# A hybrid decoder layer on one core: the order of TensorE's products turned, in the middle of each up-projection chunk and in the mixer

## The chip, the core and the metric

One core of one Trainium2 chip. The metric is device time in microseconds (us) of one execution; lower is better. The profile is taken from one execution of its own, and its span runs from the first to the last instruction.

## What is computed

One decoder layer on a sequence of 256 tokens of width 2048, in float32:

```python
h = rms_norm(x, mix_norm_g)
q, kv, gate_logits, conv_in = split(h @ w_in)
attn = nsa_attention(q, kv, sigmoid(gate_logits), ...)   # three gated branches, 16 heads of 64
conv = conformer_conv(conv_in, ...)                      # GLU, causal depthwise conv of 31 taps, LayerNorm, swish
x = x + concatenate([attn, conv]) @ w_out
h = rms_norm(x, ffn_norm_g)
u = causal_depthwise_conv(h @ w_up, ffn_conv_w, ffn_conv_b)   # 3 taps, 2 x 5632 channels
a, gate = split(u)
x = x + (silu(gate) * a) @ w_down
return rms_norm(x, final_norm_g)
```

## The kernel before

**Products in two halves.** Every operand of a large product is split into a high part, rounded to the matmul's reduced float32 form (`wh` for a weight, `xt_h` for an activation), and the rest (`wl`, `xt_l`). A product is then the sum of three: high x high, high weight x low activation, low weight x high activation. The three are accumulated in a PSUM bank, so their order is free as long as the first one starts the sum and the last one stops it. A product of TensorE has an operand that is kept (it is loaded ahead as weights, a record of its own on the row PEld) and one that streams; the width in the profile's forms (128x256, 128x512) is that of the streaming one.

**Weight chunks.** All weights stream through SBUF in chunks of 128 x 2048. The list `chunks` counts them: 0 to 2 are the head (loaded in pieces), 3 to 23 the convolution's and the keys' columns of `w_in`, 24 to 29 the values' and gates', 30 to 37 the queries', then the output projection, then 88 chunks of `w_up` and 44 of `w_down`. For each chunk the sync queue starts the load into `wraw` (3 buffers), ScalarE makes `wh` (L207), and VectorE or, for chunks 5 to 31, GpSimd makes `wl` as `wraw - wh` (L212), each in two halves in the mixer. `w_next` hands a chunk to TensorE, adds one to `st["use"]`, and writes the splitting of the chunk two ahead; the pieces are put into ScalarE's and the subtracting engine's queues in the middle of TensorE's work. There are 3 buffers of `wh` and `wl`. The order of instructions on each engine is that in which the program writes them.

**The mixer.** `tile_chunk` (L492) takes a chunk of 128 output columns and calls `mm3` (L244) for each of the 16 rows of tiles; each call issues three products of width 256 with the weight kept: `wh` x `xt_h` (L245), `wh` x `xt_l` (L246), `wl` x `xt_h` (L247). `hook` in between puts in other engines' work and ticks of the attention. At the very start the head's three chunks arrive in ten cuts (`CUTS`, `THIRD`); its products are written at L567 for the first cuts and by `mm3` for the rest, 38 calls; chunks 3 to 23 and 30 to 37 make 29 x 16 more calls. The values' products (L827 to L829) and the output projection's (L262 to L264) keep the activation and stream the weight.

**The up-projection.** For each of 22 groups m, two parts (a and gate) and two halves kh of the sum, one chunk holds 8 rows of tiles k for 2 output tiles i. Each pair (k, i) issues a product of width 512 (L1360: `wh` kept, the high and the low activation streaming side by side into the two halves of bank `bk[i]`) and one of width 256 (L1362: `wl` kept, the high activation into the first half). So the two widths take turns, and the banks change after each pair. `up_out` adds the halves of the bank afterwards, applies the three taps and the gate, and the down-projection (L254 to L257) follows.

Of the kernel before, what the change touches and what calls it, by code (L numbers as in the profile page):

```python
# [17 lines left out]
P = 128  # L18
T = 256
D = 2048  # L20
KD = D // P
# [22 lines left out]
CUTS = ((0, 1), (1, 2), (2, 4), (4, 5), (5, 6), (6, 8), (8, 10), (10, 12), (12, 14), (14, 16))  # L44
THIRD = {1: (0, 2), 2: (2, 4), 4: (4, 6), 5: (6, 8), 9: (8, 16)}
EARLY = 4


def head_of_slot(s):
# [5 lines left out]
def hybrid_trunk(ctx: ExitStack, tc: tile.TileContext, a: dict, out: bass.AP):  # L55
    nc = tc.nc
# [39 lines left out]
        presums.extend(lambda i=i: nc.gpsimd.dma_start(far, src[:, i * 512:(i + 1) * 512],  # L96
                                                       **({"accum_op": OP.add} if i else {})) for i in (0, 1, 3))

    st = {"dma": 3, "split": 3, "use": 0}
    raws, parts, pieces, halves = {}, {}, [], []  # L100
    late, lows, late_pool, far_sums, out_sums = [], [], [], {}, []
    clock = {"pe": 0.0, "dve": 0.0}
# [120 lines left out]
    def w_next(cuts=1, ahead=LA):  # L223
        c = st["use"]
        st["use"] += 1
        w_pump()
        if st["split"] >= len(chunks):
            for f in lows:
                f()
            lows.clear()  # L230
        while st["split"] <= min(c + ahead, len(chunks) - 1):
            w_pump()
            w_split(cuts)
        if cuts == 1 or POOLED[0] <= st["split"] - 1 < POOLED[1]:
            w_pump()
        now = late[:]
        late.clear()
        if now:
            clock["dve"] = max(clock["dve"], clock["pe"])
        for f in now:  # L240
            f()
        return parts.pop(c)

    def mm3(ps, wh, wl, xh, xl, first, last):  # L244
        nc.tensor.matmul(ps, wh, xh, start=first, stop=False)  # L245
        nc.tensor.matmul(ps, wh, xl, start=False, stop=False)  # L246
        nc.tensor.matmul(ps, wl, xh, start=False, stop=last)  # L247
        clock["pe"] += 0.36

    def mm_down(ps, xh, xl, wh, wl, first, last):  # L250
# [48 lines left out]
    xt = [mixp.tile([P, 4, 2, T], F32R, name="xt", bufs=4) for _ in range(4)]  # L299
    xt_h, xt_l = [[xt[k // 4][:, k % 4, i] for k in range(KD)] for i in range(2)]  # L300


    with ExitStack() as mx:
# [24 lines left out]
        for n, (lo, hi) in enumerate(CUTS):  # L328
            w = 512 * (hi - lo)
# [5 lines left out]
            if n in THIRD:  # L335
                sl = slice(*[k * P for k in THIRD[n]])
# [30 lines left out]
        for n, ((lo, hi), (xc, *wc)) in enumerate(zip(CUTS, heads)):  # L367
            xs = [(xc[:, (k - lo) * T:(k - lo + 1) * T], k) for k in range(lo, hi)]
            sl = slice(lo * P, hi * P)
            if n < EARLY:  # L370
                h, l = parts[0]
# [13 lines left out]
            if n in THIRD:  # L385
                sl = slice(*[k * P for k in THIRD[n]])
# [105 lines left out]
        def tile_chunk(ps, ticks={}, half=None):  # L492

            wh, wl = w_next(2)
            held = pieces[:] if half else []
            del pieces[:len(held)]
            for kt in range(KD):
                if kt == KD // 2 and half:
                    half()
                    pieces.extend(held)  # L500
                if kt % 4 == 2:
                    hook(kt // 4, ticks)
                sl = slice(kt * P, (kt + 1) * P)
                mm3(ps, wh[:, sl], wl[:, sl], xt_h[kt], xt_l[kt], kt == 0, kt == KD - 1)
# [53 lines left out]
        for j in range(8):  # L558
            gb, ab = [b[:, :T] for b in bank[2 * (j if j < 3 else (j + 1) % 2):][:2]]
            if j == 0:  # L560
                st["use"] = 3
                ps3 = gb, ab, bank[2][:, :T]
                for n, cut in enumerate(CUTS):
                    if n < EARLY:
                        for c, i, j in ((0, 0, 0), (0, 1, 0), (1, 0, 0), (0, 0, 1), (1, 0, 1), (1, 1, 0)):
                            for k in range(*cut):
                                nc.tensor.matmul(ps3[c], parts[c][i][:, k * P:(k + 1) * P], (xt_h, xt_l)[j][k],  # L567
                                                 start=k + i + j == 0, stop=False)
                                clock["pe"] += 0.12
                    for c, (lo, hi) in ((0, cut), (1, cut), (2, THIRD.get(n, (0, 0)))):  # L570
                        wh, wl = parts[c]
                        for k in range(lo, hi) if c == 2 or n >= EARLY else ():
                            sl = slice(k * P, (k + 1) * P)
                            mm3(ps3[c], wh[:, sl], wl[:, sl], xt_h[k], xt_l[k], k == 0, k == KD - 1)
                for c in range(3):
                    parts.pop(c)
                w_split(2)
                w_pump()
                x_squares(0, 0)
                x_squares(0, 1)  # L580
                w_split(2)
                pieces[1:3] = pieces[2:0:-1]
                w_pump(2)
                x_squares(1, 0)
                x_rstd()
                w_pump()
                first = gb, ab
                continue
# [115 lines left out]
        for n in range(4):  # L704
            kv, i = divmod(n, 2)
# [111 lines left out]
        for kh in range(2):  # L817
            wh, wl = [w.rearrange("p (k c) -> p k c", c=256) for w in w_next(2)]
            presum_step()
            for k in range(8):  # L820
                kt = kh * 8 + k
                if k % 2 == 1:
                    hook(k // 2)
                for t in range(2):
                    sl = slice(t * P, (t + 1) * P)
# [7 lines left out]
        for kq in range(4):  # L833
            wh, wl = [w[:, :4 * 304].rearrange("p (k c) -> p k c", c=304) for w in w_next(2)]
            for k in range(4):
                kt = kq * 4 + k
                hook(k)
                for t in range(2):
                    sl = slice(t * P, (t + 1) * P)
# [285 lines left out]
        def x2_tr(qr, t):  # L1125
            for k in range(4 * qr, 4 * qr + 4):
                nc.tensor.matmul(x2_at(k)[:, t * P:(t + 1) * P], x2[:, t, k * P:(k + 1) * P], ident,
                                 is_transpose=True, start=True, stop=True)

        def x2_evac(k):  # L1130
            norm_evac(x2_at(k), k, ffn_g)
# [80 lines left out]
    with ExitStack() as fx:  # L1212
# [19 lines left out]
        def g_load():  # L1232

            n = gn["n"]
            gn["n"] += 1
            if n >= NFT // 2:
                return
            q = n % (NFT // 4)
            gl = fw.tile([P, 8, P], F32R, name="gl", bufs=2)
            nc.gpsimd.dma_start(gl.bitcast(F32), gl_far[q])  # L1240
            gq.append((gh_all[:, 4 * q:4 * q + 4].rearrange("p k a t -> p (k a) t"), gl))
# [26 lines left out]
        def sum_steps():  # L1268

            for q in sums_todo[2::-1]:  # L1270
                if len(q) == 3 and any(len(r) == 3 for r in sums_todo[:sums_todo.index(q)]):
                    continue
                q.pop(0)()
            while sums_todo and not sums_todo[0]:
                sums_todo.pop(0)
# [58 lines left out]
        def up_stages():  # L1334
            for q in list(stages):
                q.pop(0)()
                if not q:
                    stages.remove(q)


        for t in range(2):
            x2_rstd(t)
        between = {(0, 1): lambda: x2_tr(3, 0), (0, 8): w_pump, (0, 9): lambda: x2_tr(3, 1),
                   (0, 10): lambda: (x2_evac(12), x2_evac(13)),
                   (0, 12): lambda: (x2_evac(14), x2_evac(15)), (1, 8): x2_spread}

        for m in range(NFT // 2):
            ya = {}
            if m == NFT // 2 - 1:
                for _ in range(2):  # L1350
                    g_load()
            for part in range(2):
                bk = UP_BANKS[2 * ((2 * m + part) % 4):][:2]
                for kh in range(2):
                    wh, wl = [w.rearrange("p (k c) -> p k c", c=256) for w in w_next(1 if m + part + kh else 2)]
                    up_stages()
                    for n, (k, i) in enumerate((k, i) for k in range(8) for i in range(2)):
                        kt = kh * 8 + k
                        sl = slice(i * P, (i + 1) * P)
                        nc.tensor.matmul(bk[i], wh[:, k, sl], xt[kt // 4][:, kt % 4].rearrange("p a t -> p (a t)"),  # L1360
                                         start=kt == 0, stop=False)
                        nc.tensor.matmul(bk[i][:, :T], wl[:, k, sl], xt_h[kt], start=False, stop=kt == KD - 1)  # L1362
                        if m + part == 0 and (kh, n) in between:
                            between.pop((kh, n))()
                up_out(m, part, bk, ya)
                sum_steps()

# [148 lines left out]
        for h in range(2):  # L1516
            nb = dict(zip((2, 3, 4, 8, 1, 5, 6, 7), ring[4 * h:] + ring[:4 * h]))
            for q in range(NQ):
# [11 lines left out]
                for j in range(2):  # L1530
                    p = 2 * q + j
# [102 lines left out]
```

## Time and profile before

| | |
|---|---|
| three runs, median (lowest to highest) | 1083.47 us (1083.26 to 1083.47) |
| the profiled execution's own time | 1083.45 us |
| its span | 1081.7 us |
| granted TensorE clock, mean | 0.999 |
| up-projection, first to last product (L1360, L1362) | 353.4 to 847.2 us |
| mixer's `mm3` products (L245, L246, L247) | 502 of each |

In the profile PE is TensorE's matmuls and PEld its weight loads, DVE VectorE, ACT ScalarE, POOL GpSimd and SP the sync engine. A row of the timeline has the start, the length, the engine, the line, the operation, and the tiles as out<-in. A matmul's length holds its way through the array and overlaps the next one's; what a product costs is the distance from its start to the next start.

### The profile page before, as it was taken

To read this page: it belongs to the slowest core of one execution; us is meant where nothing else is said; L and a number is where in the kernel's file an instruction comes from. 1 tells how busy PE (TensorE), PEld (TensorE's weight loads), DVE (VectorE), ACT (ScalarE), POOL (GpSimd) and SP (SyncE) were. 2 spreads that over 40 slices of the span, in tenths; PEclk is the share of its full clock that TensorE was granted. 3 is DMA by queue.
4 is the path that set the end of the run, shared out by engine and by line. 5 is a ranking of instruction groups with operands and counts; after the bars stand their busy time and mean duration, and the time that the engine had idled before them with its cause. 6 is when DMAs were issued, how large, how long until landed. Compare 5 with 4: busy or idle time off the path is not lost.

```text
span 1081.7 us, 17521 instructions
## 1 busy us (share of the span) xinstructions
PE 1071.9 (99%) x6721; PEld 956.4 (88%) x6721; DVE 897.7 (83%) x1429; ACT 620.2 (57%) x895; POOL 368.0 (34%) x420
## 2 busy tenths in 40 slices
PE   9999999999999999999999999999999999999997
PEld 9999999998888888888888888888888888888886
DVE  6799986787895677777787878888787899999997
ACT  7534456778664545555455655555555555555563
POOL 0888975758000202333323433211121222211220
PEclk9999999999999999999999999999999999999999
DMA  9776756322565969999999999866668699979882
GB/s 354 243 262 253 222 145 237 115 90 107 198 219 206 279 213 277 272 290 262 307 278 292 287 289 301 272 217 219 224 224 270 210 394 343 345 287 351 324 314 99
DMA packets 62016, 272.82 MB, mean 252 GB/s; under 512 B 8187, under 2 KB 11531, under 8 KB 42348
## 3 DMA queue, kind: packets, MB, share of 16 engines
q1 hardware_dynamic: 34748, 199.33, 51.3%
q0 software_dynamic: 23536, 65.29, 22.6%
q10 hardware_dynamic: 3648, 7.08, 1.8%
q8 instruction: 53, 0.87, 0.3%
q14 instruction: 31, 0.25, 0.1%
HBM read 254.87 MB, written 41.18 MB: 274 GB/s over the span
## 4 chain that ended last, share of the span: by engine, by line
PE 97%; DVE 2%; issue 0%; POOLq 0%; POOL 0%; DVEq 0%
PE bank L1360 30%; PE bank L1362 15%; PE bank L254 6%; PE bank L256 6%; PE bank L247 5%; PE bank L245 5%; PE bank L246 5%; PE bank L257 3%; PE bank L255 3%; PE bank L262 3%; PE bank L264 3%; PE bank L263 3%; PE bank L1015 1%; PE bank L992 1%; PE bank L947 1%; PE bank L948 0%
## 5 line engine op out<-in xcount | busy, mean ns | idle before, releaser
L1360 PE MATMUL bank<-xt,wh 128*128 128x512 f32 x1408 | 493.0, 395 | 0.0
L207 ACT ACTIVATE wh<-wraw 128x1024 fp32r<-128x1024 f32 (+2 forms) x187 | 263.7, 1432 | 276.7 <-PE bank L1360 121.2
L1362 PE MATMUL bank<-xt,wl 128*128 128x256 f32 x1408 | 394.9, 280 | 0.0
L212 DVE TENSOR_TENSOR wl<-wraw,wh 128x2048 fp32r<-128x2048 f32 (+1 forms) x133 | 254.4, 1918 | 108.6 <-ACT wh L207 108.6
L1360 PEld LDWEIGHTS bank<-xt,wh 128*128 128x128 f32 x1408 | 264.7, 188 | 61.2
L1362 PEld LDWEIGHTS bank<-xt,wl 128*128 128x128 f32 x1408 | 264.3, 188 | 0.1
L247 PE MATMUL bank<-xt,wl 128*128 128x256 f32 x502 | 142.1, 283 | 0.0
L245 PE MATMUL bank<-xt,wh 128*128 128x256 f32 x502 | 141.8, 282 | 0.0
L246 PE MATMUL bank<-xt,wh 128*128 128x256 f32 x502 | 140.9, 281 | 0.0
L212 POOL TENSOR_TENSOR wl<-wraw,wh 128x1024 fp32r<-128x1024 f32 (+1 forms) x54 | 122.4, 2320 | 16.7 <-ACT wh L207 16.5
L129 DVE TENSOR_TENSOR wl<-wraw,wh 128x2048 fp32r<-128x2048 f32 x44 | 100.4, 2285 | 4.7 <-ACT wh L128 4.7
L245 PEld LDWEIGHTS bank<-xt,wh 128*128 128x128 f32 x502 | 94.6, 188 | 1.5 <-issue 0.9
L247 PEld LDWEIGHTS bank<-xt,wl 128*128 128x128 f32 x502 | 94.4, 188 | 0.5 <-POOL wl L212 0.2
L246 PEld LDWEIGHTS bank<-xt,wh 128*128 128x128 f32 x502 | 94.2, 188 | 0.4
L524 DVE SCALAR_TENSOR_TENSOR bank<-us,cw,bank 128x256 f32<-128x256 f32 x232 | 93.4, 481 | 0.7 <-ACT bank L519 0.2
L1265 POOL DMA_DIRECT2D sum<-in_w_d x84 | 64.0, 833 | 73.1 <-issue 49.5
L128 ACT ACTIVATE wh<-wraw 128x2048 fp32r<-128x2048 f32 x44 | 82.8, 1903 | 7.8 <-PE bank L1360 4.1
L128 ACT ACTIVATE xh<-sums 128x1536 fp32r<-128x1536 f32 x28 | 41.8, 1492 | 78.8 <-DVE sums L157 56.4
L1299 DVE SCALAR_TENSOR_TENSOR yt<-u,fcw,yt 128x255 f32<-128x255 f32 (+1 forms) x176 | 81.0, 481 | 3.1
L1330 POOL DMA_DIRECT2D glf<-glt x22 | 12.9, 587 | 194.1 <-DVE glt L129 136.7
L256 PE MATMUL bank<-wl,gh 128*128 128x512 f32 x167 | 65.7, 393 | 0.0
L254 PE MATMUL bank<-wh,gh 128*128 128x512 f32 x167 | 65.6, 393 | 0.0
(308 smaller groups left out, 1872.3 us busy)
## 6 DMA issues: line engine op xcount, KB each, us to landing
wraw<-in_w_u SPq DMA_DIRECT2D x88, 1024.0 KB, 7.4
wraw<-in_w_t SPq DMA_DIRECT2D x28, 1024.0 KB, 5.1
sum<-in_w_d POOLq DMA_DIRECT2D x84, 256.0 KB, 8.5
wraw<-in_w_d SPq DMA_DIRECT2D x28, 768.0 KB, 6.9
wraw<-in_w_d SPq DMA_DIRECT2D x16, 1024.0 KB, 7.5
gs<-gsf POOLq DMA_DIRECT2D x56, 256.0 KB, 6.7
wraw<-in_w_o SPq DMA_DIRECT2D x13, 1024.0 KB, 4.8
gl<-glf POOLq DMA_DIRECT2D x22, 512.0 KB, 5.5
```

Of the source, the lines that this page charges most:

```text
L128: nc.scalar.activation(hi, src, AF.Copy)
L129: return lambda: nc.vector.tensor_sub(lo, src, hi.bitcast(F32))
L207: nc.scalar.activation(h[:, sl], raw[:, sl], AF.Copy)
L212: (nc.gpsimd if pooled else nc.vector).tensor_sub(l[:, sl], raw[:, sl], h[:, sl].bitcast(F32))
L245: nc.tensor.matmul(ps, wh, xh, start=first, stop=False)
L246: nc.tensor.matmul(ps, wh, xl, start=False, stop=False)
L247: nc.tensor.matmul(ps, wl, xh, start=False, stop=last)
L254: nc.tensor.matmul(ps, xh, wh, start=first, stop=False)
L256: nc.tensor.matmul(ps, xh, wl, start=False, stop=False)
L524: nc.vector.scalar_tensor_tensor(y[:, j] if last else acc[0], us[:, j, k:k + T], cw[:, j, k:k + 1], acc[0], op0=OP.mult, op1=OP.add)
L1360: nc.tensor.matmul(bk[i], wh[:, k, sl], xt[kt // 4][:, kt % 4].rearrange("p a t -> p (a t)"), start=kt == 0, stop=False)
L1362: nc.tensor.matmul(bk[i][:, :T], wl[:, k, sl], xt_h[kt], start=False, stop=kt == KD - 1)
```

## The change

Two orders of products are turned; the sums stay the same up to the order of addition.

In the mixer, `mm3` takes the three products in an order from a table. The row of the table is `st["use"] % 4`, which is one more than the chunk's number, and the two entries of a row alternate from call to call (the second entry is taken first). Product 0 is high x high, 1 is `wh` x low activation, 2 is `wl` x high activation:

```diff
+ROUNDS = (((0, 1, 2), (0, 1, 2)), ((0, 2, 1), (0, 2, 1)), ((0, 1, 2), (2, 1, 0)), ((0, 1, 2), (1, 2, 0)))
+TURNS = (lambda w, s, l: ((w, 4), (l, 4), (l, 5), (w, 5)),
+         lambda w, s, l: ((w, 4), (w, 5), (l, 4), (l, 5)),
+         lambda w, s, l: ((w, 4), (l, 4), (w, 5), (l, 5)),
+         lambda w, s, l: ((l, 4), (l, 5), (w, 4), (w, 5)),
+         lambda w, s, l: ((s, 4), (l, 4), (w, 5), (l, 5)))
...
     def mm3(ps, wh, wl, xh, xl, first, last):
-        nc.tensor.matmul(ps, wh, xh, start=first, stop=False)
-        nc.tensor.matmul(ps, wh, xl, start=False, stop=False)
-        nc.tensor.matmul(ps, wl, xh, start=False, stop=last)
+        pairs = ((wh, xh), (wh, xl), (wl, xh))
+        st["odd"] ^= 1
+        for n, i in enumerate(ROUNDS[st["use"] % len(ROUNDS)][st["odd"]]):
+            nc.tensor.matmul(ps, *pairs[i], start=first and n == 0, stop=last and n == 2)
```

In the up-projection the 16 pairs of a chunk are written as a list of calls, `whole(j)` for the 512-wide product and `low(j)` for the 256-wide one. From m = 1 on, the four products of the pairs 4 and 5 (the third row of tiles, banks 0 and 1) are put in one of five orders. The fifth uses `split(j)`, which makes the 512-wide product as two 256-wide ones with the same weight:

```diff
+                    def split(j):
+                        k, i = divmod(j, 2)
+                        for n, x in enumerate((xt_h, xt_l)):
+                            nc.tensor.matmul(bk[i][:, n * T:(n + 1) * T], wh[:, k, i * P:(i + 1) * P], x[kh * 8 + k],
+                                             start=False, stop=False)
...
+                    order = [(f, j) for j in range(16) for f in (whole, low)]
+                    if m:
+                        order[8:12] = TURNS[(4 * m + 2 * part + kh) % len(TURNS)](whole, split, low)
+                    for f, j in order:
+                        f(j)
```

The lists of the other engines keep their order. TensorE's list before, where chunk 4 (bank 4) ends and chunk 5 (bank 5) begins; a number behind a name is the buffer's, and the square brackets name the engine that the product waits for:

```order
L245 MATMUL bank_68<-xt,wh 128x256
L246 MATMUL bank_68<-xt,wh 128x256
L247 MATMUL bank_68<-xt,wl 128x256
L245 MATMUL bank_69<-xt,wh 128x256 [waits Activation_49]
L246 MATMUL bank_69<-xt,wh 128x256
L247 MATMUL bank_69<-xt,wl 128x256 [waits Pool_49]
```

The same place now (all three products stand on line 256 of the changed kernel; x2, x3 and x4 are so many alike in a row):

```order
L256 MATMUL bank_68<-xt,wl 128x256
L256 MATMUL bank_68<-xt,wh 128x256
L256 MATMUL bank_69<-xt,wl 128x256 [waits Pool_49]
L256 MATMUL bank_69<-xt,wh 128x256 [waits Activation_49]
L256 MATMUL bank_69<-xt,wh 128x256 x3
L256 MATMUL bank_69<-xt,wl 128x256 x2
```

In chunk 4 the product with `wl` has moved from the last place of three to the middle. In chunk 5 it has moved to the first, so that the wait for GpSimd's `wl` now stands ahead of that for ScalarE's `wh`; in the next call it is last again.

The second place is TensorE's list in the up-projection, in the first chunk of m = 1 (banks 6 and 7), which takes the fifth order. Before, from the fourth pair to the seventh:

```order
L1360 MATMUL bank_71<-xt,wh 128x512
L1362 MATMUL bank_71<-xt,wl 128x256
L1360 MATMUL bank_70<-xt,wh 128x512
L1362 MATMUL bank_70<-xt,wl 128x256
L1360 MATMUL bank_71<-xt,wh 128x512
L1362 MATMUL bank_71<-xt,wl 128x256
```

And now (line 1369 is `whole`, 1375 `split`, 1381 `low`):

```order
L1369 MATMUL bank_71<-xt,wh 128x512
L1381 MATMUL bank_71<-xt,wl 128x256
L1375 MATMUL bank_70<-xt,wh 128x256 x2
L1381 MATMUL bank_70<-xt,wl 128x256
L1369 MATMUL bank_71<-xt,wh 128x512
L1381 MATMUL bank_71<-xt,wl 128x256
```

One 512-wide product has become two 256-wide ones; the rest of the chunk stands as before.

More of the change, by code (lines that the diff above doesn't have):

```diff
@@ L97, in presum @@
                                                        **({"accum_op": OP.add} if i else {})) for i in (0, 1, 3))
-    st = {"dma": 3, "split": 3, "use": 0}
+    st = {"dma": 3, "split": 3, "use": 0, "odd": 0}
     raws, parts, pieces, halves = {}, {}, [], []
@@ L1356, in hybrid_trunk, with whole, low @@
                     up_stages()
-                    for n, (k, i) in enumerate((k, i) for k in range(8) for i in range(2)):
+                    def whole(j):
+                        k, i = divmod(j, 2)
                         kt = kh * 8 + k
[L1359 to L1364, printed above, removed]
+                        nc.tensor.matmul(bk[i], wh[:, k, i * P:(i + 1) * P],
+                                         xt[kt // 4][:, kt % 4].rearrange("p a t -> p (a t)"), start=kt == 0, stop=False)
+                    def split(j):
+                        k, i = divmod(j, 2)
+                        for n, x in enumerate((xt_h, xt_l)):
+                            nc.tensor.matmul(bk[i][:, n * T:(n + 1) * T], wh[:, k, i * P:(i + 1) * P], x[kh * 8 + k],
+                                             start=False, stop=False)
+                    def low(j):
+                        k, i = divmod(j, 2)
+                        kt = kh * 8 + k
+                        nc.tensor.matmul(bk[i][:, :T], wl[:, k, i * P:(i + 1) * P], xt_h[kt], start=False, stop=kt == KD - 1)
+                    order = [(f, j) for j in range(16) for f in (whole, low)]
[3 more added lines that the diff above has]
+                        f(j)
+                        if m + part == 0 and f is low and (kh, j) in between:
+                            between.pop((kh, j))()
                 up_out(m, part, bk, ya)
```

## Prediction

> **What bounds the kernel now.** I read the page first, then the wait lists of TensorE and of its weight loads, then the timeline of TensorE at the places that the change touches. From the page, the span, TensorE's row, and the first two lines of the chain that ended last:
>
> ```profile
> span 1081.7 us, 17521 instructions
> PE 1071.9 (99%) x6721; PEld 956.4 (88%) x6721; DVE 897.7 (83%) x1429; ACT 620.2 (57%) x895; POOL 368.0 (34%) x420
> PE 97%; DVE 2%; issue 0%; POOLq 0%; POOL 0%; DVEq 0%
> PE bank L1360 30%; PE bank L1362 15%; PE bank L254 6%; PE bank L256 6%; PE bank L247 5%; PE bank L245 5%; PE bank L246 5%; PE bank L257 3%; PE bank L255 3%; PE bank L262 3%; PE bank L264 3%; PE bank L263 3%; PE bank L1015 1%; PE bank L992 1%; PE bank L947 1%; PE bank L948 0%
> ```
>
> TensorE is the path: 97% of the chain. So the time is the number of products times their spacing, plus the few places where TensorE waits. The busy means of the matmul groups (395 and 280 ns) overlap, so the spacing has to come from start to start. In the up-projection the timeline shows four records of one bank pair, with the weight loads between them (columns: start, length, engine, line):
>
> ```profile
> 399.71 0.40 PE L1360 MATMUL bank<-xt,wh 128*128 128x512 f32 x1
> 399.94 0.28 PE L1362 MATMUL bank<-xt,wl 128*128 128x256 f32 x1
> 399.94 0.19 PEld L1360 LDWEIGHTS bank<-xt,wh 128*128 128x128 f32 x1
> 400.06 0.40 PE L1360 MATMUL bank<-xt,wh 128*128 128x512 f32 x1
> 400.06 0.19 PEld L1362 LDWEIGHTS bank<-xt,wl 128*128 128x128 f32 x1
> 400.29 0.28 PE L1362 MATMUL bank<-xt,wl 128*128 128x256 f32 x1
> ```
>
> A 512-wide product takes 0.23 us to the next start, a 256-wide one 0.12. The load of the next weights starts with the running product, so it is under it. Over the whole stage the spacing never breaks; the stage's first product, and the first one behind it, are
>
> ```profile
> 353.43 0.39 PE L1360 MATMUL bank<-xt,wh 128*128 128x512 f32 x1
> ...
> 847.36 0.40 PE L254 MATMUL bank<-wh,gh 128*128 128x512 f32 x1
> ```
>
> With 1408 pairs that is (847.36 - 353.43) / 1408 = 0.3508 us a pair, and 0.23 + 0.12 = 0.35: no wait is left in the stage.
>
> **The up-projection's turns.** From m = 1 on there are 21 x 2 x 2 = 84 chunks, numbered 4 to 87 by 4m + 2part + kh; by five that is 17 each for remainders 4, 0, 1 and 2 and 16 for remainder 3. Remainder 2 is the old order. The others put 256-wide products next to each other, or 512-wide ones, where before they took turns. Does a spacing depend on the neighbour? In the mixer 256-wide follows 256-wide, 27 products from the first to the last row; and so in the value projection, where the operand that is kept changes places with the one that streams:
>
> ```profile
> 66.09 0.28 PE L245 MATMUL bank<-xt,wh 128*128 128x256 f32 x1
> 66.21 0.28 PE L246 MATMUL bank<-xt,wh 128*128 128x256 f32 x1
> 66.33 0.28 PE L247 MATMUL bank<-xt,wl 128*128 128x256 f32 x1
> ...
> 69.27 0.28 PE L245 MATMUL bank<-xt,wh 128*128 128x256 f32 x1
> ```
>
> ```profile
> 154.02 0.28 PE L827 MATMUL bank<-wh,xt 128*128 128x256 f32 x1
> 154.13 0.28 PE L828 MATMUL bank<-wl,xt 128*128 128x256 f32 x1
> ...
> 157.20 0.28 PE L827 MATMUL bank<-wh,xt 128*128 128x256 f32 x1
> ```
>
> Both give 3.18 / 27 = 0.1178 us. 512-wide behind 512-wide, in the output projection, from first to last row five products:
>
> ```profile
> 336.25 0.39 PE L263 MATMUL bank<-wl,ma_h 128*128 128x512 f32 x1
> ...
> 337.41 0.40 PE L262 MATMUL bank<-wh,ma_h 128*128 128x512 f32 x1
> ```
>
> 1.16 / 5 = 0.232, what is left of a pair: 0.3508 - 0.1178 = 0.233. So a product costs what its width costs, whoever is before or behind it, and the turns with the same four products (50 chunks) cost 0. Both weight halves are whole before the chunk's first pair has passed, since that pair reads both, so a turn at the fifth and sixth pair adds no wait. Remainder 4 replaces a 512-wide product by two 256-wide ones: 2 x 0.1178 - 0.233 = +0.003 us each, 17 of them +0.05 us.
>
> Here a rule speaks against the change. The load's row on the page is
>
> ```profile
> L1362 PEld LDWEIGHTS bank<-xt,wl 128*128 128x128 f32 x1408 | 264.3, 188 | 0.1
> ```
>
> so a split adds 17 loads of 188 ns; if they stood on the path that would be 17 x 0.188 = +3.2 us, and hidden they are nothing. The trace says hidden: the load at 399.94 is still running (0.19) when the next product starts at 400.06. I take 0. The Trainium skill, page "TensorE: Matmul & The Clock Gate", section "The mechanism" (Part 3), states that a weight load overlaps running matmuls only where its row group differs, and all products here use the full array. By that rule the sum would have the +3.2 us; the trace disagrees with it. It stands below as a rival.
>
> **The mixer's three products.** The counter of chunks is one ahead, so chunks c with c mod 4 = 0 take (0,2,1) for all products, c mod 4 = 1 alternates (2,1,0) with (0,1,2), c mod 4 = 2 alternates (1,2,0) with (0,1,2), c mod 4 = 3 stays; the head (38 calls) is set to 3 and so takes the (1,2,0) pair. Of the 29 chunks of 16 calls, 7, 7, 7 and 8 fall in these classes: 112 + 56 + 56 + 19 = 243 of 502 calls change. All are 256 wide, so their spacing costs 0; read to 0.01 us over 27 products, the rows leave at most 0.001 us either way for each of 3 x 243 products, +-0.7 us, which I keep for the range.
>
> What does cost is need: wl is made last, and orders that start with product 2 ask for it two products sooner. The wait list of the weight loads has two such waits in the whole kernel:
>
> ```profile
> PEld bank L247 <- POOL wl L212: 0.2, 1, 0.2
> PEld bank L247 <- DVE wl L358: 0.2, 1, 0.2
> ```
>
> The second is in the head (chunk 0, k = 6), the first at the start of chunk 5:
>
> ```profile
> 35.55 0.28 PE L245 MATMUL bank<-xt,wh 128*128 128x256 f32 x1
> 35.67 0.28 PE L246 MATMUL bank<-xt,wh 128*128 128x256 f32 x1
> 35.94 0.39 PE L247 MATMUL bank<-xt,wl 128*128 128x256 f32 x1
> 36.17 0.28 PE L245 MATMUL bank<-xt,wh 128*128 128x256 f32 x1
> ```
>
> ```profile
> 33.49 26.05 POOL L212 TENSOR_TENSOR wl<-wraw,wh 128x1024 fp32r<-128x1024 f32 x11 [1.65 <-ACT wh L207]
> ```
>
> GpSimd's eleven half-chunk subtractions take 26.05 / 11 = 2.37 us each, so the first half of chunk 5's wl is there at 33.49 + 2.37 = 35.86, and TensorE's L247 starts at 35.94. Chunk 5 has 5 mod 4 = 1: now L247 comes first. It can start no sooner than 35.94, and the other two, which ran in the wait before, come behind it: 2 x 0.1178 = **+0.24 us**. Delays ahead of that are swallowed there. In the head the new order leaves one product more behind the wait, +0.12; in chunk 4's second half (0,2,1) does the same, at most +0.12, where L247 is late by 0.04:
>
> ```profile
> 32.50 0.36 PE L245 MATMUL bank<-xt,wh 128*128 128x256 f32 x1
> 32.70 0.28 PE L246 MATMUL bank<-xt,wh 128*128 128x256 f32 x1
> 32.86 0.39 PE L247 MATMUL bank<-xt,wl 128*128 128x256 f32 x1
> ```
>
> Together they bring TensorE to chunk 5 at no later than 35.55 + 0.24 = 35.79, still before 35.94; GpSimd's subtraction hangs on the landed chunk and ScalarE, not on these products. From then on wl gains: two subtractions take 4.74 us and a chunk 48 x 0.1178 = 5.65, so each chunk adds 0.9 us of lead, and two products' 0.24 us are covered. If that cover were gone, each chunk start would cost what chunk 5's does.
>
> Is the 0.24 us given back where TensorE later waits? Its longest late wait is in the attention, and the chain in order of time shows what it hangs on:
>
> ```profile
> 193.22 0.13 PE bank L948
> 193.37 0.29 DVE e L957
> ...
> 202.28 0.39 PE bank L947
> ```
>
> VectorE's run there starts from TensorE's own L948, so it comes later by as much and nothing is given back. Nor does another engine's list change; a buffer's last reader moves by at most one product (0.12 us).
>
> **Sum.** +0.24 + 0.05 + 0 = +0.29 us. The profiled execution took 1083.45 us (span 1081.7), the median of the three runs is 1083.47, so they are the same: 1083.5 + 0.3 = **1083.8 us**, span 1082.0. A measurement of this kernel can tell about 0.2% (2.2 us) from no change: forecast, no change.
>
> **Rivals.**
> 1. *wl is late everywhere (slower).* If wl's lead were under two products at each half of the mixer's turned chunks, the 7 chunks of class 1 would lose 2 x 7 x 0.236 = 3.3 us and the 14 of classes 0 and 2, one product each, 2 x 14 x 0.118 = 3.3: 1083.5 + 6.6 = 1090.1. It decides from a lead below 0.24 us; ten such waits pass 0.2%. For it: chunk 5's lead is below zero. Against it: the lead grows by 0.9 us a chunk, and the wait list has no other. Chance 0.03.
> 2. *A load is not hidden (slower).* The 17 added loads stand on the path: 1083.8 + 3.2 = 1087.0. For it: a load's 0.19 us is longer than a 256-wide spacing, and a split puts three 256-wide products behind each other. Against it: the mixer does that all the time at 0.1178. By the rule of the Trainium skill's page above this would be the outcome; the trace bears it out nowhere. Chance 0.02.
> 3. *A turned order runs closer (faster).* If the turned products kept the shortest spacing of the rows, 0.11 (154.02 to 154.13), they would save 3 x 243 x 0.008 = 5.8 us: 1078.0. Against it: in the same rows the next spacing is 0.12, and every run of 27 gives the same mean. Chance 0.02.
> 4. *It does nothing at all*: a later wait swallows chunk 5's delay, and the time is 1083.5. For it: TensorE does wait at 202.28. Chance 0.05.
>
> **How the numbers follow.** Forecast 0.88. Its low end is 1083.8 - 0.7 for the spacing and -0.2 for the spread of the runs (1083.26 to 1083.47): 1082.9. Its high end is 1083.8 + 0.7 + 0.24, one more wait like chunk 5's, + 0.2: 1084.9, rounded to 1085.0. That also holds rival 4; rivals 1 to 3 lie outside. Faster by over 0.2% is rival 3, 0.02; slower is rivals 1 and 2, 0.05; within it, 0.93.
>
> **What would show it.** Span 1082.0; the up-projection's first to last product 493.93 us longer by 0.05; in chunk 5 the wl product first at 35.94 with two behind it, and every later chunk 0.24 us later; the split's two products 0.12 apart. Wrong would be a pair of turned products 0.19 or more apart for 256-wide ones, a wl wait in a chunk after 5, or an up-projection shorter or longer than 493.9 by over 0.7 us.

## The result, and the profile after

The changed kernel takes 1076.16 us (median of three runs, 1076.11 to 1076.20) against 1083.47 before: a ratio of 0.9933, interval 0.9911 to 0.9956. The forecast was 1083.8 with 1082.9 to 1085.0, and no change. The gain of 7.3 us was not foreseen.

From the page of the changed kernel, the lines that answer to those of before:

```profile
span 1074.3 us, 17561 instructions
PE 1064.4 (99%) x6738; PEld 952.7 (89%) x6738; DVE 898.0 (84%) x1429; ACT 621.3 (58%) x895; POOL 366.8 (34%) x420
PE 95%; DVE 2%; DMA 1%; ACT 1%; issue 0%; SPq 0%; POOLq 0%; POOL 0%; DVEq 0%
```

TensorE has 17 products more, is as full as before (99%), and is still the path. So the time did not come out of a wait: the same products lie closer together. The groups of the up-projection, of before and then of after, say where (the last number ahead of the second bar is the mean length of one, in ns):

```profile
L1360 PE MATMUL bank<-xt,wh 128*128 128x512 f32 x1408 | 493.0, 395 | 0.0
L1362 PE MATMUL bank<-xt,wl 128*128 128x256 f32 x1408 | 394.9, 280 | 0.0
```

```profile
L1369 PE MATMUL bank<-xt,wh 128*128 128x512 f32 x1391 | 474.9, 392 | 0.0
L1381 PE MATMUL bank<-xt,wl 128*128 128x256 f32 x1408 | 380.7, 278 | 0.0
```

Even the mean length has dropped, by 3 and 2 ns. The stage's first product, and the first one behind it, in the timeline of after:

```profile
353.53 0.39 PE L1369 MATMUL bank<-xt,wh 128*128 128x512 f32 x1
...
840.01 0.39 PE L263 MATMUL bank<-wh,gh 128*128 128x512 f32 x1
```

840.01 - 353.53 = 486.48 us, where before had 493.93. The difference, 7.45 us, is the whole gain (span 1081.7 to 1074.3: 7.4). Everything ahead of the stage and behind it is as long as it was.

The view that shows it best counts products in a stretch of fixed length (columns: window, its length, PE busy with the number of products, granted clock, DMA share, GB/s). Before, then after:

```profile
380.00:580.00 200.00, 200.00 (x1145) 1.00 0.92 272
```

```profile
380.00:580.00 200.00, 200.00 (x1171) 1.00 0.92 276
```

The granted clock is 1.00 in both, so it is not the clock. TensorE is busy all the time in both, so no view of waits can show it. 1145 products in 200 us are 0.350 us a pair, where a pair is one 512-wide and one 256-wide product (200 x 2 / 0.350 = 1143, and those at the window's ends).

Where do pairs run closer? The starts of six chunks in a row in after, numbers 9 to 14, each row a chunk's first product:

```profile
404.50 0.40 PE L1369 MATMUL bank<-xt,wh 128*128 128x512 f32 x1
...
410.10 0.40 PE L1369 MATMUL bank<-xt,wh 128*128 128x512 f32 x1
...
415.60 0.39 PE L1369 MATMUL bank<-xt,wh 128*128 128x512 f32 x1
...
421.07 0.39 PE L1369 MATMUL bank<-xt,wh 128*128 128x512 f32 x1
...
426.51 0.39 PE L1369 MATMUL bank<-xt,wh 128*128 128x512 f32 x1
...
432.06 0.40 PE L1369 MATMUL bank<-xt,wh 128*128 128x512 f32 x1
```

The five chunks take 5.60, 5.50, 5.47, 5.44 and 5.55 us, 27.56 in all; before, each takes 5.60 (16 x 0.350), 28.0 in all. The fourth, 5.44, is chunk 12, whose number leaves 2 by five: *the old order*, unchanged, and the fastest. 5.44 / 16 = 0.340 us a pair. So it is not the turned products that run closer. The unturned pairs behind them do; the turn only passes them from one spacing to the other. The cycle repeats through the stage: 0.44 us in five chunks, for 84 chunks, is 7.4.

### The profile page after: what moved, and what is told of

It reads as the page before. It is cut to its first block, busy times and chain, and to the rows that moved or that the text cites. A ratio compares the mean times of both kernels' runs of the same rounds, so it can differ in the third digit from the quotient of the medians.

```text
span 1074.3 us, 17561 instructions
## 1 busy us (share of the span) xinstructions
PE 1064.4 (99%) x6738; PEld 952.7 (89%) x6738; DVE 898.0 (84%) x1429; ACT 621.3 (58%) x895; POOL 366.8 (34%) x420
## 4 chain that ended last, share of the span: by engine, by line
PE 95%; DVE 2%; DMA 1%; ACT 1%; issue 0%; SPq 0%; POOLq 0%; POOL 0%; DVEq 0%
PE bank L1369 30%; PE bank L1381 15%; PE bank L256 15%; PE bank L263 6%; PE bank L265 6%; PE bank L266 3%; PE bank L264 3%; PE bank L271 3%; PE bank L273 3%; PE bank L272 3%; PE bank L1024 1%; PE bank L1001 1%; DMA hb<-in_head 1%; PE bank L956 1%; PE bank L957 0%
## 5 line engine op out<-in xcount | busy, mean ns | idle before, releaser
L1369 PE MATMUL bank<-xt,wh 128*128 128x512 f32 x1391 | 474.9, 392 | 0.0
L1381 PE MATMUL bank<-xt,wl 128*128 128x256 f32 x1408 | 380.7, 278 | 0.0
L1369 PEld LDWEIGHTS bank<-xt,wh 128*128 128x128 f32 x1391 | 257.7, 188 | 51.9
L1381 PEld LDWEIGHTS bank<-xt,wl 128*128 128x128 f32 x1408 | 263.2, 188 | 4.3
L256 PE MATMUL bank<-xt,wh 128*128 128x256 f32 x1004 | 177.2, 281 | 0.0
L256 PEld LDWEIGHTS bank<-xt,wh 128*128 128x128 f32 x1004 | 151.0, 188 | 0.8
L256 PE MATMUL bank<-xt,wl 128*128 128x256 f32 x502 | 132.6, 284 | 0.1
L256 PEld LDWEIGHTS bank<-xt,wl 128*128 128x128 f32 x502 | 91.6, 188 | 1.7 <-issue 0.9
L992 POOL TENSOR_SCALAR e<-e,lsum 128x128 f32<-128x128 f32 x64 | 55.8, 888 | 22.8 <-ACT qs L879 14.7
L1256 POOL DMA_DIRECT2D gs<-gsf x56 | 30.6, 549 | 74.0 <-PE bank L266 71.9
```

The lines of the kernel that those rows point to most:

```text
L256: nc.tensor.matmul(ps, *pairs[i], start=first and n == 0, stop=last and n == 2)
L1369: nc.tensor.matmul(bk[i], wh[:, k, i * P:(i + 1) * P], xt[kt // 4][:, kt % 4].rearrange("p a t -> p (a t)"), start=kt == 0, stop=False)
L1381: nc.tensor.matmul(bk[i][:, :T], wl[:, k, i * P:(i + 1) * P], xt_h[kt], start=False, stop=kt == KD - 1)
```

## What before already showed

The two spacings stand in the trace of before, on the same line with the same widths. From its timeline, around the two `x2_spread` products (L1208, which stand as four records) in the second chunk:

```profile
361.50 0.39 PE L1360 MATMUL bank<-xt,wh 128*128 128x512 f32 x1
...
361.84 0.39 PE L1360 MATMUL bank<-xt,wh 128*128 128x512 f32 x1
...
362.18 0.39 PE L1360 MATMUL bank<-xt,wh 128*128 128x512 f32 x1
...
362.87 0.61 PE L1208 MATMUL bank<-dg,ones 128*128 128x128 f32 x4
...
363.66 0.40 PE L1360 MATMUL bank<-xt,wh 128*128 128x512 f32 x1
...
364.01 0.40 PE L1360 MATMUL bank<-xt,wh 128*128 128x512 f32 x1
...
364.36 0.40 PE L1360 MATMUL bank<-xt,wh 128*128 128x512 f32 x1
```

Ahead of L1208 a pair takes 0.34 us, and the product's own length reads 0.39; behind it 0.35 and 0.40. From 363.66 to the end of the stage, some 1380 pairs, nothing returns to 0.34. The trace keeps its times in nanoseconds, which the rows above round to ten. In these the short rhythm is 226 or 227 + 113 or 114 ns, every pair alike, with each weight load 3 or 4 ns behind the start of the product that runs. The long one is 232 or 233 + 117 or 118, and it is a pattern of *two* pairs: the load that starts with the 512-wide product starts in turn 2 or 3 and 5 ns behind it.

That gave the theory: **a run of equal pairs keeps one of two rhythms, 0.340 or 0.350 us, until a small shift in time passes it to the other.** Its rivals: the turned order is itself what runs closer; the mixer has a share in it; a product costs its width, as predicted.

## Experiments

Each time is that of one run, and the time of the kernel before beside it is from the same chip; where a range is given, it is a median of several. An edit is shown against the changed kernel, if nothing else is said; from the one-turn run on the mixer's table is also set back as in the first edit, which is not shown again, but for the runs with an alternating mixer.

**The up-projection's turns alone**, the mixer in its old order:

```diff
-ROUNDS = (((0, 1, 2), (0, 1, 2)), ((0, 2, 1), (0, 2, 1)), ((0, 1, 2), (2, 1, 0)), ((0, 1, 2), (1, 2, 0)))
+ROUNDS = (((0, 1, 2), (0, 1, 2)),)
```

> The up-projection's turns as in the change, the mixer's three products in the old order everywhere. Theory (rhythm): a run of equal pairs keeps one of two rhythms, 0.340 or 0.350 us a pair, and a turn can pass it from one to the other; the whole gain is the chunks at 0.340, 7.4 us by the profile of after, so about 1076.1 us. Rival (mixer): the mixer's orders bring the gain, so about 1083.5 us.

Measured: 1076.49 us (before 1083.34). The gain is the up-projection's: 6.85 us on this chip, and from its first product to the first one behind it the stage takes 486.48 us, as in the changed kernel.

**The mixer's orders alone**, the up-projection in its old order:

```diff
-                    if m:
+                    if False:
```

> The mixer's orders as in the change, the up-projection in the old order. Rhythm: the mixer's share is after less the run with the up-projection's turns alone, 1076.16 - 1076.49 = -0.3 us, so about 1083.1 us, with the up-projection at 0.350 a pair. The prediction's sum for the mixer alone: +0.24, 1083.7 us. If the mixer brought the gain after all: 1076.

Measured: 1083.88 us (before 1083.49), +0.4. At the start of chunk 5 the forecast wait is there, in its list of weight loads' waits and its timeline:

```profile
PEld bank L256 <- POOL wl L220: 0.4, 1, 0.4
```

```profile
35.49 0.28 PE L256 MATMUL bank<-xt,wh 128*128 128x256 f32 x1
35.92 0.39 PE L256 MATMUL bank<-xt,wl 128*128 128x256 f32 x1 [0.15 <-POOL wl L220]
36.14 0.63 PE L256 MATMUL bank<-xt,wh 128*128 128x256 f32 x4
```

The `wl` product comes first, at 35.92, and the call's other two behind it, 36.14 and one more: with 0.117 us each, the next call starts at 36.38 where before had 36.17. That is 0.21 us more. Counted from the end of GpSimd's subtraction, 33.46 + 2.40 = 35.86 here, the next call starts 0.51 us behind it, where before had 0.28 (36.17 - 35.89): 0.23 us more, and the forecast was 0.24. In the changed kernel itself little of the wait is left: GpSimd's subtraction, which began at 33.49 in the trace of before, begins at 33.17 in that of after and is done at 33.17 + 2.40 = 35.57, ahead of chunk 5's first product. That product's weight load starts at 35.63, and the product behind it comes 0.18 us later instead of 0.12, a slip of 0.06 us:

```profile
33.17 4.77 POOL L220 TENSOR_TENSOR wl<-wraw,wh 128x1024 fp32r<-128x1024 f32 x2 [2.03 <-ACT wh L215]
...
35.63 0.19 PEld L256 LDWEIGHTS bank<-xt,wl 128*128 128x128 f32 x1
```

```profile
35.67 0.34 PE L256 MATMUL bank<-xt,wl 128*128 128x256 f32 x1
35.85 0.64 PE L256 MATMUL bank<-xt,wh 128*128 128x256 f32 x4
```

In the traces of all runs it began between 32.82 and 33.87 us, and of those that leave chunk 5 in its old order it was done from 0.33 us ahead of the chunk's first product (the run with both, at the end) to 0.80 us behind it (the cut in chunk 41): the head moves by more from run to run than the term that was forecast. The changed kernel against its up-projection alone is 1076.16 - 1076.49 = -0.3, the mixer alone +0.4: its share is within 0.4 us of nothing.

**One turn instead of 67**: only chunk 4 takes the order w4 l4 l5 w5 (w is a pair's 512-wide product, l its 256-wide one, with the pair's number); the mixer is old.

```diff
-                    if m:
-                        order[8:12] = TURNS[(4 * m + 2 * part + kh) % len(TURNS)](whole, split, low)
+                    if 4 * m + 2 * part + kh == 4:
+                        order[8:12] = TURNS[0](whole, split, low)
```

> The old order everywhere but for one turn in the whole kernel: chunk 4 of the up-projection takes the first of the five orders (wide 4, narrow 4, narrow 5, wide 5). Rhythm: before chunk 4 the pairs run at 0.350, behind the turn all pairs to the end of the stage at 0.340: some 83.6 chunks x 16 pairs x 0.010 us = 13.4 us less, about 1070.1 us, nearly twice the gain of the 67 turns. Rival (cheaper products): a turn's own four products are cheaper, 7.3 us / 67 = 0.1 us for one turn, so about 1083.4 us.

Measured: 1070.59 us (before 1083.34). One turned group of four products, of 1408 pairs, gives 12.75 us, nearly twice what 67 give. The counts of products by stretch, ahead of the spread, behind it, and behind the turn:

```profile
355.00:362.00 7.00, 7.00 (x44) 1.00 0.81 242
364.00:378.00 14.00, 14.00 (x82) 1.00 1.03 295
380.00:833.00 453.00, 453.00 (x2667) 1.00 0.86 271
```

The first stretch also holds four small products that are no pairs. 453 x 2 / 2667 = 0.3397 us a pair to the end of the stage. The turned order as the source of the gain is out: it stands in the stage once.

**There and back**: the same turn in chunk 4, and the fourth order (l4 l5 w4 w5), which in the changed kernel always passes from 0.340 to 0.350, in chunk 40.

> Two turns in the whole kernel: the first of the five orders in chunk 4 of the up-projection, as in the run with one turn, and the fourth (narrow 4, narrow 5, wide 4, wide 5) in chunk 40. In the profile of after that order passed the rhythm from 0.340 to 0.350 each time. Rhythm: 0.340 from chunk 4 to 40, 0.350 behind it; the run with one turn plus 47.6 x 16 x 0.010 = 7.6 us, 1078.2 us. If a turn were good by itself: 1070.6 us or less.

Measured: 1077.83 us (before 1083.49). Between the turns, and behind the second:

```profile
380.00:573.00 193.00, 193.00 (x1137) 1.00 0.93 279
576.00:840.00 264.00, 264.00 (x1511) 1.00 0.80 258
```

0.3395 and 0.3494 us a pair. A turn costs or gains by what it leaves behind, and in both directions.

**The spread one pair later**, to see whether 0.350 hangs on where the spread falls (the kernel before with (1, 9) for (1, 8)):

> The kernel before without any turned product; only the two small products that spread the norm's factor over the partitions stand one pair later in chunk 1 of the up-projection (behind pair 9 instead of pair 8). In the profile of before the pairs run at 0.340 until these products and at 0.350 ever after. Rhythm: what follows depends on where the disturbance falls; if the later place leaves the pairs at 0.340, 1083.5 - 86.6 x 16 x 0.010 = 1069.6 us, if not, 1083.5. Rival (cheaper products): nothing is turned, so 1083.5 us and 0.350.

Measured: 1083.60 us (before 1083.34). The 0.340 lasts one pair longer, up to the spread, and 0.350 follows again.

**Products added, nothing turned**: extra products ahead of seven chunks, into a bank that the chunk's first product starts afresh (work that the sums do not use).

```diff
-                    if m:
-                        order[8:12] = TURNS[(4 * m + 2 * part + kh) % len(TURNS)](whole, split, low)
...
+                    for wide in {4: (256,), 12: (256, 256), 20: (256,) * 3, 28: (512,), 36: (512, 512), 44: (128,),
+                                 52: (128, 128)}.get(4 * m + 2 * part + kh, ()):
+                        nc.tensor.matmul(bk[0][:, :wide], wh[:, 0, :P], xt[0][:, 0].rearrange("p a t -> p (a t)")[:, :wide],
+                                         start=True, stop=True)
```

> No pair is turned anywhere. Ahead of chunk 4 of the up-projection one more narrow product is issued into the bank that the chunk is about to start (its result is overwritten), ahead of chunk 12 two, of chunk 20 three, of chunk 28 one wide, of chunk 36 two wide, of chunk 44 one of width 128, of chunk 52 two of those. Theory (rhythm, passed over by a shift in time): the order is only one way to shift the pairs, so at least one of the seven kicks also passes the rhythm to 0.340 or back, and the stage from there runs at it; if the first does and it is never passed back, about 1070.6 + 2.5 us for the added products, 1073. Rival (order): only products in another order do it; all pairs stay at 0.350 and the time is 1083.5 + 2.5 = 1086 us.

Measured: 1078.68 us (before 1083.49): *more* work, 4.8 us less time. By stretch, behind the first, fourth, fifth, sixth and seventh:

```profile
380.00:420.00 40.00, 40.00 (x237) 1.00 0.75 238
...
510.00:551.00 41.00, 41.00 (x243) 1.00 1.00 302
555.00:595.00 40.00, 40.00 (x230) 1.00 0.96 300
600.00:640.00 40.00, 40.00 (x238) 1.00 0.99 301
645.00:840.00 195.00, 195.00 (x1116) 1.00 0.74 246
```

One 256-wide product passed from 0.350 to 0.340 (80 / 237 = 0.338); two and three of them and one of 512 left it there; two of 512 passed back to 0.350 (80 / 230 = 0.348); one of 128 passed to 0.340; two of 128 passed back. No order of the pairs is needed, only a shift. Nor does the DMA share decide: it is 0.75 and 0.99 in two stretches at 0.340 (the first and the fourth row), and 0.96 in the one at 0.350 between them.

**What decides whether a shift passes.** A cut product (`split`) is the smallest shift that the change holds. In chunk 4, cut pair 5, or pair 4, or 6, or 7; and pair 4 in chunk 41. The edit of the first, and of the second, each in place of the turns:

```diff
+                    if 4 * m + 2 * part + kh == 4:
+                        order[10:11] = [(split, 5)]
```

```diff
+                    if 4 * m + 2 * part + kh == 4:
+                        order[8:9] = [(split, 4)]
```

> One split in the whole kernel: in chunk 4 of the up-projection pair 5's wide product is made as two narrow ones. In the profile of after a split at pair 4 passed the rhythm from 0.350 to 0.340 in chunk 4, but left it at 0.350 in chunks 9, 14 and on, where the slow rhythm's two-pair pattern stood one pair off. Rhythm: a split at pair 5 in chunk 4 meets the pattern one pair off, so it stays at 0.350: 1083.5 us. If any split gives the fast rhythm, 1070.1 us. Rival (cheaper products): 1083.5 us either way.

> The kernel before with one edit in the up-projection: in its fifth chunk (m = 1, part = 0, kh = 0) the 512 wide product of pair 4 is issued as two of 256, as the change does it in 17 chunks. Nothing is turned. Theory (two rhythms that a run of equal pairs keeps, 0.340 and 0.350 us a pair; what passes from one to the other is a small shift in time at a certain place): in the changed kernel this same cut at this same chunk passed to 0.340, so here it does too, and 84 chunks of 16 pairs then run about 9.7 ns a pair closer: 13.0 us less, 1070.6 us. Rival (only an order with two products of one weight part behind each other passes; a cut product never does): all pairs stay at 0.350, 1083.5 us.

> The kernel before with one product cut in two, as in the runs with pair 4 (which passed to 0.340 us a pair) and pair 5 (which stayed at 0.350), now at pair 6 of the same chunk, the up-projection's fifth. Theory (the 0.350 rhythm is a pattern of two pairs: the loads that start with the 512 wide product start in turn 3 and 5 ns behind it, and a cut passes only at a pair of the one kind): pair 6 is of the kind of pair 4, so all pairs behind it run at 0.340: 1070.2 us. Rival (what decides is the distance from the chunk's start, or the bank: pair 4 alone, or the first tiles alone, pass): stays at 0.350, 1083.5 us.

> The same with pair 7, which writes the other bank. Theory (pattern of two pairs): pair 7 is of the kind of pair 5, so it stays at 0.350 us a pair: 1083.6 us. Rival (distance from the chunk's start: pair 5 was an exception): passes to 0.340, 1070.3 us.

> The cut at pair 4 again, but in the up-projection's chunk 41, that is 37 chunks of 16 pairs later. Theory (pattern of two pairs, kept without a slip through the stage): 37 x 16 pairs is an even number, so the pair is of the kind that passes, and the 747 pairs behind it run 9.7 ns closer: 7.2 us less, 1076.3 us. Rival (the pattern slips on the way, or the chunk's half decides): stays at 0.350, 1083.5 us.

Measured, in this order: 1083.70, 1070.19, 1070.12, 1083.32 and 1076.20 us (before: 1083.34 for the first, 1083.60 as a median of seven for the second, 1083.06 for the others). From the windows of pair 5, of pair 4, of pair 6, of pair 7, and of pair 4 in chunk 41 (which begins at 584 us):

```profile
380.00:580.00 200.00, 200.00 (x1145) 1.00 0.91 272
```

```profile
380.00:580.00 200.00, 200.00 (x1179) 1.00 0.93 280
```

```profile
380.00:580.00 200.00, 200.00 (x1179) 1.00 0.93 280
```

```profile
380.00:580.00 200.00, 200.00 (x1145) 1.00 0.91 272
```

```profile
380.00:580.00 200.00, 200.00 (x1145) 1.00 0.92 272
600.00:800.00 200.00, 200.00 (x1179) 1.00 0.82 262
```

1145 is 0.350 a pair, 1179 is 0.340. The even pairs pass, the odd ones do not, and an even one passes 37 chunks later too. In the nanoseconds the cuts that pass stand where the load is due 2 or 3 ns behind the product, those that do not where it is due 5 (in the runs with pairs 5 and 7 it came 6 behind). Even pairs also write the first of the chunk's two banks and odd ones the second, so these five runs alone leave the bank as a rival. The changed kernel settles that: all of its 17 cuts are at pair 4, in the first bank. The first (chunk 4, a load 3 ns behind) passes to 0.340; that of chunk 9, behind the l4 l5 w4 w5 of the chunk before, meets the other place (5 ns behind) and stays at 0.350, and so do those after it, since their chunks take the same 5.60 us. So what decides is the place in the pattern of two pairs.

**Every second pair from 3 to 13 turned**, in all chunks from m = 1 on:

```diff
-                    order = [(f, j) for j in range(16) for f in (whole, low)]
-                    if m:
-                        order[8:12] = TURNS[(4 * m + 2 * part + kh) % len(TURNS)](whole, split, low)
+                    order = [(f, j) for j in range(16) for f in ((whole, low), (low, whole))[m > 0 and j % 2 and 1 < j < 15]]
```

> No single turn but all: from m = 1 on, in every chunk, the pairs 3, 5, 7, 9, 11 and 13 give their 256 wide product ahead of the 512 wide one, the others as before, so that two 512 and two 256 wide products alternate through most of a chunk. Theory (a rhythm belongs to a run of equal groups, and the products themselves cost the same in any order): this order has a rhythm of its own that no run has shown, between the two known ones: 1070.6 us (0.340 a pair) to 1083.5 us (0.350); I take the middle of what single turns of this kind gave (chunks with w w l l 5.473 us against 5.440 and 5.600), 1073 us. Rival (the turned order is what runs close, and each turned group gains for itself): well below the one turn's 1070.6 us, 1066 us or less.

Measured: 1079.29 us (before 1083.60, median of seven), between the two bounds, but above the 1073 that was taken as the middle. Its rhythm is its own, 400 / 1154 = 0.347:

```profile
380.00:580.00 200.00, 200.00 (x1154) 1.00 0.92 272
```

Turned groups do not run closer than 0.340: six in each chunk are slower than none, once the 0.340 is reached.

**The best of it**: the one turn two chunks earlier (chunk 2); the mixer's products in alternating orders, with the turn at chunk 4; and both, with the old order in chunk 10 and 22.

> The kernel before with one turned group (w4 l4 l5 w5) in the up-projection's third chunk (m = 0, part = 1, kh = 0), two chunks ahead of where the one-turn run had it; nothing else is changed. Theory (one passage into the 0.340 rhythm, kept to the stage's end): the chunks 3 and 4 now run at 0.340 as well, some 30 pairs by 9.7 ns, 0.3 us less than the one turn at chunk 4: 1070.3 us, and every pair from about 366 us on at 0.340. If this group, at this place, does not pass: 1083.5 us, as before. Rival (a product costs its width in any order, as predicted): 1083.5 us, all pairs at 0.350.

> One turn in the up-projection as in the run with one turn (1070.6 us), and in the mixer from chunk 6 on all calls alternate (2,1,0) and (0,1,2), which in the profile of after ran at 0.1156 us a product in chunks 9, 13 and 17, and at 0.1184 in chunks 5 and 21, against 0.1178 in the old order. Rhythm: the 26 chunks keep one of the two; at the fast one 26 x 48 x 0.0022 = 2.7 us less, 1067.9 us, at the slow one 0.8 more, 1071.4. Rival (width alone): 1070.6 us.

> The early single turn, and in the mixer the three products of a call in the orders (2, 1, 0) and (0, 1, 2) by turns in chunks 6 to 9 and 11 to 21, with chunks 10 and 22 and the rest in the old order (0, 1, 2), since the run with the alternating mixer held 115.56 ns a product in chunks 6 to 9 and lost it to 117.8 in chunk 10. Theory (rhythms in the mixer too, each kept until something shifts it, and an old-order chunk sets it back to where the alternating order runs close): 15 chunks of 48 calls' products, 720 by 2.2 ns, 1.6 us less than the early turn alone: 1068.7 us. If chunk 10 does not set it back, only chunks 6 to 9 gain, 192 products by 2.2 ns, 0.4 us, with what the loss of an even start costs or gives: 1069.9 us. Rival (the mixer's order is worth nothing): 1070.3 us.

Measured: the early turn 1070.06 us (median of four, 1069.68 to 1070.56), against 1083.60 before (median of seven, 1082.68 to 1085.47): ratio 0.9878, interval 0.9861 to 0.9894, with 0.340 from 367.7 us on. The turn at chunk 4 with the alternating mixer: 1069.81 us (before 1083.49), neither of the two times that the theory gave (1067.9 and 1071.4), since the mixer did not keep one rhythm. Both together: 1069.32 us (median of four, 1069.15 to 1069.55), ratio 0.9870, interval 0.9855 to 0.9884; so the 0.7 us between the last and the early turn are not told apart by the intervals. The mixer has rhythms as well; chunks 6 to 8, and those from 10 on, in the early turn alone and then in both together:

```profile
41.60:58.00 16.40, 16.40 (x142) 1.00 0.61 208
65.50:120.00 54.50, 54.50 (x465) 1.00 0.71 249
```

```profile
41.60:58.00 16.40, 16.40 (x145) 1.00 0.61 204
65.50:120.00 54.50, 54.50 (x465) 1.00 0.71 248
```

In chunks 6 to 9 the alternating order takes 0.1156 us a product, the old one 0.1178. From chunk 10 on both take 0.1178, and so it is where all chunks from 6 on alternate. The old-order chunk that was to set the close rhythm back did not do so: instead of the 1.6 us of 15 chunks there is the 0.4 us of four (192 products by 2.2 ns).

## Why the prediction was wrong, point by point

- **The failed step**: "So a product costs what its width costs, whoever is before or behind it, and the turns with the same four products (50 chunks) cost 0." The stage took 7.45 us less, where the forecast had +0.05. The first half of the sentence holds within 3%, and these 3% are 13 us here. What a product costs is the rhythm that the run is in, and a turn acts on all the pairs behind it. The step divided the stage by its pairs (0.3508) and read one pair at 400 us. That mean is 1380 pairs at 0.350 and a few at 0.340; the rows at 361 us, on the same line, show both. The neighbouring pairs were costed, not those far behind.
- **The splits**, "+0.003 us each": each cut itself costs 0.003 to 0.004 us (chunk 9 takes 5.603 for 5.600). Right as a price, beside the point: one cut moved 13 us.
- **The loads**: no load of a split came onto the path. Two half-wide products start 118 to 123 ns apart, with 188 ns loads under them. The rule of the Trainium skill, page "TensorE: Matmul & The Clock Gate", section "The mechanism", that a load overlaps only where its row group differs, is contradicted by these starts as by those of before, if it is read without an exception, as the prediction read it. The same section names one, a load into "the background weight buffer"; no trace here shows into which buffer a load goes. Rival 2 did not happen.
- **The mixer**, "0, +-0.7 us": right in sum, not in its reason. In after, the class that alternates (2,1,0) with (0,1,2) runs at 0.1157 in chunk 9, while the next one runs at 0.1188 in chunk 10:

```profile
59.01 0.40 PE L256 MATMUL bank<-xt,wl 128*128 128x256 f32 x2
...
62.48 0.40 PE L256 MATMUL bank<-xt,wl 128*128 128x256 f32 x2
```

```profile
66.23 0.28 PE L256 MATMUL bank<-xt,wl 128*128 128x256 f32 x1
...
69.08 0.28 PE L256 MATMUL bank<-xt,wl 128*128 128x256 f32 x1
```

That is 30 products in 3.47 us, and 24 in 2.85. The classes cancel: in the trace, chunks 9, 13 and 17 are together 0.30 us shorter than before, and chunks 6, 10, 14, 18, 21 and 22 together 0.27 us longer. The bound of 0.001 us a product was too narrow for a class (+-0.002) and held for the whole.
- **Chunk 5's wait**, +0.24: confirmed in the mixer alone, down to 0.06 us in the changed kernel's trace, where `wl` was done 0.1 us ahead of the chunk's first product. The prediction took this distance from one execution, and it differs by 1.1 us between the runs.
- **Rival 3**, "A turned order runs closer", had the sign but the wrong place and mechanism: it put 0.008 us on the mixer's turned products. The chance of faster, 0.02, rested on two short runs of rows with the same mean, and no longer run was counted. Rival 1 did not happen: the list of after's weight loads' waits holds none for GpSimd's `wl`, and the one delay that the rows show is chunk 5's 0.06 us. Rival 4 is out by its time.
- Of "what would show it", "an up-projection shorter ... by over 0.7 us" was the line that decided: 7.45 us.

Open: why the pairs lock into these two spacings, and why 2 or 3 ns of offset let a shift pass and 5 do not. The traces show the starts and not what TensorE waits for between them, and no run here took the weight loads away.

## What to carry to other kernels

Where an engine is busy all the time, count its instructions per 100 us along the stage, and compare stretches of the same code: a mean over the stage hides two rhythms that differ by 3%. If both occur, look for what passes from one to the other, and place one shift there instead of many; then a change in order is costed by the rhythm it leaves behind, not by the products it turns. Whether other products have such rhythms is not shown here; the count tells.

## What the runs showed of the chip

At a granted clock of 1.00, a run of products of 512 and 256 columns in turn, each with its own weight load, holds 0.340 us a pair (227 + 113 ns) or 0.350 (233 + 117) for hundreds of pairs, through chunk ends and changes of bank. The 0.350 rhythm was ended by one extra product of 128 or 256 columns, by one turned group, and by one cut if it fell on the right one of two pairs; in the 0.340 rhythm two or three of 256 or one of 512 did nothing, two of 512, two of 128 or the turned group l4 l5 w4 w5 ended it. It is not chance: in the changed kernel the five chunks' times repeat to 2 ns from cycle to cycle, from the second cycle on. A run of 256-wide products has its own: 0.1156, 0.1178 and 0.1188 us were each kept over whole chunks.
